# Placing the tiles of a hybrid attention block on multiples of 64 bytes

## Chip, core and metric

The kernel runs on one core of one Trainium2 chip. The metric is the time of one execution on the device in microseconds (us); lower is better. Three executions of the kernel before were timed, and one more was profiled.

## What is computed

One decoder block on 512 tokens of width 2048, in float32. The input is normalised and projected; half of the width goes to eight heads of 128 with compressed, selected and windowed attention (two key and value groups), the other half to sixteen heads of 64 with a window of 128 and an attention sink. Both are gated, projected back, added to the input and normalised.

```python
h = _rmsnorm(x, norm_g[l])
proj = h @ w_in[l]
(qa, kca, vca, ksa, vsa, kwa, vwa, za, ga, qb, kb, vb, zb) = jnp.split(proj, offsets, axis=-1)
...
o_cmp, p_cmp = _compressed_attention(qa, kc, vc)
sel_idx = _select_blocks(p_cmp, S)
o_sel = _selected_attention(qa, _rope(_heads(ksa, N_KV_A, HEAD_DIM_A)), _heads(vsa, N_KV_A, HEAD_DIM_A), sel_idx)
o_win = _banded_attention(qa, _rope(_heads(kwa, N_KV_A, HEAD_DIM_A)), _heads(vwa, N_KV_A, HEAD_DIM_A), WIN_A)
o_a = gates[..., 0:1] * o_cmp + gates[..., 1:2] * o_sel + gates[..., 2:3] * o_win
y_a = o_a.reshape(B, S, WIDTH_A) * jax.nn.silu(za)
o_b = _banded_attention(qb, _rope(_heads(kb, N_KV_B, HEAD_DIM_B)), _heads(vb, N_KV_B, HEAD_DIM_B),
                        WIN_B, sink=sinks[l].reshape(N_KV_B, GROUP_B))
y_b = o_b.reshape(B, S, WIDTH_B) * jax.nn.silu(zb)
x = x + jnp.concatenate([y_a, y_b], axis=-1) @ w_out[l]
return _rmsnorm(x, final_g)
```

With 512 tokens and blocks of 64 there are eight blocks, fewer than the sixteen that are selected, so every block is selected.

## The kernel before

**Three matmuls for one product.** Each float32 operand is split into a rounded word (`hi`, type float32r) and the rest (`lo`). `mm3` forms a product from three float32r matmuls, and these are lines 113 to 115 of the profile:

```python
def mm3(ps, ah, al, bh, bl, first, last, go_on=False):
    pe.matmul(ps, ah, bh, start=first, stop=False, skip_group_check=go_on)
    pe.matmul(ps, ah, bl, start=False, stop=False, skip_group_check=go_on)
    recent["mm"] = pe.matmul(ps, al, bh, start=False, stop=last, skip_group_check=go_on).ins
```

The operand `a` is loaded into TensorE as weights (128 columns), `b` is the moving operand that streams past it. In the profile's names the moving and the loaded operand both stand behind the arrow, moving first: `pj<-xh,whi` streams `xh` past weights `whi`, and `oa<-whi,yh` streams weight words past `yh`.

**Stages.** Weights come from memory by SP's queue into raw tiles (`raw`, 128 x 1024), ScalarE rounds them into `whi` (L89, L616, L913) and VectorE takes the difference into `wlo` (L90, L617, L914); three buffers each. The stages in order of time, with the window that the profile shows:
- to about 96 us: x is loaded, scaled and split into `xh` and `xl` (64 KB a partition in all), and two passes form keys and values to be compressed, and the keys of the other branches, 512 columns a matmul (`bank`, `pj`).
- 96 to 174 us: values token by token, weight words moving in 256 or 408 columns past slices of x, mixed with the two compressions (L228, L229 against the tiles `F`).
- to 201 us: gate and query projections of the first head.
- 201 to 416 us: heads of the first group (`pair` and `attn_a`). A head's query and gate are formed by seven products instead of eight, 256 columns each, from combined tiles `pu`, `xh`, `xl` and, late, halves of the key tiles. In between stand scores (L539), transposes through TensorE (L577, L589, L591), and products with values (L583 to L585).
- 416 to 655 us: the second group, sixteen heads two by two (`qb_evac`, `softmax_b`, `attn_b`): 512-column projections, scores of 256 columns (L820, L821), transposes (L855).
- 655 to 828 us: the output. 512 columns in the first quarter (to 704 us), then for each other quarter seven products of 256 columns with weight words moving past `yh`, `yl` and combinations of them; the raw words of some are summed by a second transfer that accumulates (`ch`, `rw`), or by VectorE (L1072, L1154).

**Order.** A scheduler orders the instructions of each engine by a model of their times, with a few orders fixed by hand (`issue_after`); engines work in that order and wait for each other by semaphores.

**Places in SBUF.** Tiles come from pools that are stacked from the left and from the right end of each partition; a tile's place follows from the sizes opened before it, rounded to 32 bytes. The constants (`ident`, `tab`, `rstd`, `rstdb`, `gates`, `gt`, `eps`) come first, then `wp` with the raw and the split weight words, then `yp` (eight tiles of 4 KB: `F`, `pu`, later the attention's outputs), then work tiles. On the right lie x, and below it keys and values. Three constants have sizes that are no multiple of 64 bytes: `tab` with its single column `rowvalid` at the end (3588 bytes), `rstd` (16) and `eps` (4).

In the built program before, these places follow (bytes from a partition's start, mod 256): weight words 160, `F` and `pu` 160, x and `yh` 224, first key tile (`KH0`, `KL0`) 224, second (`KH1`, `KL1`) 96, `ph` and `pl` 32, queries 160, keys of the second group (`KBH`) 96. All are 32 mod 64.

**Small tiles.** The softmax keeps a minimum (`mn`) and a denominator (`dn`) per row, in the second group also the sink's term (`ex`); each is a tile of 16 or 24 bytes with two buffers.

Of the kernel before, what the change touches and what calls it, by code (L numbers as in the profile page):

```python
# [10 lines left out]
F32 = mybir.dt.float32  # L11
# [6 lines left out]
P = 128  # L18
S = 512
D = 2048  # L20
KT = D // P
NQ = S // P
# [5 lines left out]
CMP = 32  # L28
WARM = 40
FIRST = 1  # L30
TAB_W = 512 + NQ * CMP + 256 + 1


@with_exitstack
def hybrid_block(ctx, tc, xT, xtm, w0, w1s, w2s, wz, wq, wkb, wo0, wos, cw1, cw2, cpos, rope, tabs, sinks, gT, fg, out):
# [3 lines left out]
    def sb(name, bufs=1, side=None):  # L39
        return tc.tile_pool(name=name, bufs=bufs, side=side)  # L40

    const = ctx.enter_context(sb("const"))
    wp = ctx.enter_context(sb("wp", bufs=3))
    ident = const.tile([P, P], F32, name="ident")
    make_identity(nc, ident)
    tab = const.tile([P, TAB_W], F32, name="tab")
    dmask = tab[:, 0:512]
    cmask = tab[:, 512:512 + NQ * CMP]
    bmask = tab[:, 512 + NQ * CMP:768 + NQ * CMP]
    rowvalid = tab[:, TAB_W - 1:TAB_W]  # L50
    rstd = const.tile([P, NQ], F32, name="rstd")
    rstdb = const.tile([P, S], F32, name="rstdb")
    gates = const.tile([P, NQ, 24], F32, name="gates")
    gt = const.tile([P, KT], F32, name="gt")

    def dram(name, *shape):
        return tc.dram_tile(list(shape), F32, name=name)
# [5 lines left out]
    fd = dram("fd", 4, 2, P, KT // 4, 256)  # L63
    fw = dram("fw", 2, 2, P, KT // 4, 256)
    yd = [dram(f"yd{h}", P, S) for h in range(8)]
    eps = const.tile([P, 1], F32, name="eps")
    dve.memset(eps, EPS)
    act.activation(rstd[:, 0:1], eps, AF.Copy)

# [11 lines left out]
    def load_unit(src, width, rawp=None, opening=False):  # L81
# [9 lines left out]
                                       op=ALU.subtract).ins  # L91
        return hi, lo

    xstack = ctx.enter_context(ExitStack())
    xpool = xstack.enter_context(sb("xpool", side="right"))
    xh = xpool.tile([P, KT, S], F32R, name="xh")
# [23 lines left out]
        last["rope"] = dve.tensor_tensor(out=t2[64:128], in0=ps[0:64], in1=sin[0:64], op=ALU.mult).ins  # L120
        return t1, t2

    yp = ctx.enter_context(sb("yp"))
    p0 = ExitStack()
    s0 = p0.enter_context(sb("s0"))
    s0b = p0.enter_context(sb("s0b", bufs=2))
# [376 lines left out]
    wk = wks.enter_context(sb("wk", bufs=2))  # L503
# [8 lines left out]
    sA = ExitStack()  # L512
    pss = sA.enter_context(tc.tile_pool(name="pssA", bufs=1, space=PSUM, side="right"))
    wa = sA.enter_context(sb("wa"))

    def attn_a(h, qh, ql, st):
        g = h // 4
# [2 lines left out]
        pc = wa.tile([P, NQ, 4, CMP], F32, name="pc", tag="pc")  # L520
        for pair in range(2):
            tt = wa.tile([P, 1792 if pair else 768], F32, name=f"tt{pair}", tag=f"tt{pair}")
            mn = wk.tile([P, 2, 3], F32, name="mn", tag="mn")
            dn = wk.tile([P, 2, 3], F32, name="dn", tag="dn")
            views = []
            off = 0
            for i in range(2):
# [221 lines left out]
    psb = ctx.enter_context(ExitStack())  # L749
    pssb = psb.enter_context(tc.tile_pool(name="pssB", bufs=2, space=PSUM, side="right"))  # L750
    wb = wbs.enter_context(sb("wb"))
    cosB, sinB = cosA, sinA
    nc.sync.dma_start(cosB, rope[:, 2, :])
    nc.sync.dma_start(sinB, rope[:, 3, :])
# [48 lines left out]
    def softmax_b(i, q2):  # L803
        g = i // 4
        tts = []
        skb = sk[:, 0, 2 * i:2 * i + 2].unsqueeze(1).to_broadcast([P, 2, 2])
        nskb = sk[:, 1, 2 * i:2 * i + 2].unsqueeze(1).to_broadcast([P, 2, 2])
        for part in range(2):
            mn = wk.tile([P, 2, 2], F32, name="mnb", tag="mnb")
            dn = wk.tile([P, 2, 2], F32, name="dnb", tag="dnb")  # L810
            ex = wk.tile([P, 2, 2], F32, name="exb", tag="exb")
            for e in range(2):
                qt = 2 * part + e
                tt = wb.tile([P, 2, 256], F32, name="ttb", tag="ttb", bufs=6)
                tts.append(tt)
                ko = max(qt - 1, 0) * P
                qs = slice(qt * P, (qt + 1) * P)
                sp = pssb.tile([P, 2, 256], F32, name="spb", tag="spb")
                for v in range(2):
                    pe.matmul(sp[:, v, :], q2[v][:, qs], KBH[:, g, ko:ko + 256], start=v == 0, stop=False)  # L820
                    pe.matmul(sp[:, v, :], q2[v][:, qs], KBL[:, g, ko:ko + 256], start=False, stop=v == 1)  # L821
                n = 256 if qt else 128
                for v in range(2):
                    dve.tensor_tensor_reduce(out=tt[:, v, 0:n], in0=sp[:, v, 0:n], in1=bmask[:, 256 - n:256],
                                             scale=-SCALE_B, scalar=1e38, op0=ALU.add, op1=ALU.min,
                                             accum_out=mn[:, e, v:v + 1])
            dve.tensor_tensor(out=mn, in0=mn, in1=nskb, op=ALU.min)  # L827
            dve.tensor_tensor(out=ex, in0=mn, in1=skb, op=ALU.add)
            act.activation(ex, ex, AF.Exp)
            for e in range(2):  # L830
                n = 256 if part or e else 128
                for v in range(2):
                    tv = tts[2 * part + e][:, v, 0:n]
                    act.activation(tv, tv, AF.Exp, bias=mn[:, e, v:v + 1], scale=-1.0, accum_out=dn[:, e, v:v + 1])  # L834
            dve.tensor_tensor(out=dn, in0=dn, in1=ex, op=ALU.add)
            dve.reciprocal(dn, dn)
            for e in range(2):
                n = 256 if part or e else 128
                for v in range(2):
                    tv = tts[2 * part + e][:, v, 0:n]  # L840
                    dve.tensor_scalar(tv, tv, dn[:, e, v:v + 1], None, op0=ALU.mult)
        return tts
# [404 lines left out]
def _tables():  # L1247
    def rope(d):
        inv = np.float32(10000.0) ** (-np.arange(0, d, 2, dtype=np.float32) / np.float32(d))
        ang = np.arange(S, dtype=np.float32)[None, :] * inv.astype(np.float32)[:, None]  # L1250
        return np.cos(ang.astype(np.float64)).astype(np.float32), np.sin(ang.astype(np.float64)).astype(np.float32)

    ca, sa = rope(128)
    cb, sb_ = rope(64)
    cb, sb_ = np.concatenate([cb, cb]), np.concatenate([sb_, sb_])
    ro = np.stack([np.concatenate([ca, ca]), np.concatenate([sa, -sa]),
                   np.concatenate([cb, cb]), np.concatenate([sb_, -sb_])], axis=1).astype(np.float32)
    p = np.arange(P)[:, None]
    j = np.arange(P)[None, :]
    caus = np.where(j <= p, 0.0, NEG)  # L1260
    band = np.where(j > p, 0.0, NEG)
    c = np.arange(CMP)[None, :]
    cm = [np.where((16 * c + 31 <= q * P + p) & (c < 31), 0.0, NEG) for q in range(NQ)]
    tabs = np.concatenate([np.zeros((P, 384)), caus] + cm + [band, caus, (p >= 31) * 1.0], axis=1).astype(np.float32)
    return np.ascontiguousarray(ro), np.ascontiguousarray(tabs)


# [51 lines left out]
```

## Time and profile before

| | |
|---|---|
| median of 3 executions | 831.02 us (827.9 to 832.21) |
| the profiled execution's own time | 829.19 us |
| its span, first to last instruction | 827.4 us |
| granted TensorE clock, mean | 0.997 |
| TensorE busy | 811.5 us, 98% of the span |
| VectorE, ScalarE, GpSimd busy | 662.1, 485.6 and 89.3 us |
| moved by DMA | 128.30 MB |

A matmul's listed duration runs from its start to its modelled end; the next one starts earlier than that, so durations overlap and the distance between starts is what a matmul costs. Weight loads (PEld) overlap matmuls. An engine's idle time counts only where the chain of work that ended last goes through it.

### The profile page before, as it was taken

To read this page: it belongs to the slowest core of one execution; us is meant where nothing else is said; L and a number is where in the kernel's file an instruction comes from. 1 tells how busy PE (TensorE), PEld (TensorE's weight loads), DVE (VectorE), ACT (ScalarE), POOL (GpSimd) and SP (SyncE) were. 2 spreads that over 40 slices of the span, in tenths; PEclk is the share of its full clock that TensorE was granted. 3 is DMA by queue.
4 is the path that set the end of the run, shared out by engine and by line. 5 is a ranking of instruction groups with operands and counts; after the bars stand their busy time and mean duration, and the time that the engine had idled before them with its cause. 6 is when DMAs were issued, how large, how long until landed. Compare 5 with 4: busy or idle time off the path is not lost.

```text
span 827.4 us, 14161 instructions
## 1 busy us (share of the span) xinstructions
PE 811.5 (98%) x5278; PEld 735.6 (89%) x5278; DVE 662.1 (80%) x1311; ACT 485.6 (59%) x1026; POOL 89.3 (11%) x69
## 2 busy tenths in 40 slices
PE   9999999999999999999999999999999999999996
PEld 7788898999999999999888888888888788999996
DVE  6869786966799898999766688877677798877895
ACT  6734456564676786787665365645444647554555
POOL 3600002011001001101011121011011000110000
PEclk9999999999999999999999999999999999999998
DMA  9665885898330222522733321222222226797845
GB/s 324 194 206 166 281 290 200 265 371 284 103 111 22 99 77 92 166 90 89 251 107 102 99 92 56 74 80 74 77 76 77 77 62 241 235 251 198 244 96 203
DMA packets 52117, 128.30 MB, mean 155 GB/s; under 512 B 4945, under 2 KB 17233, under 8 KB 52049
## 3 DMA queue, kind: packets, MB, share of 16 engines
q1 hardware_dynamic: 50032, 120.59, 43.3%
q0 software_dynamic: 1728, 6.29, 4.3%
q8 instruction: 41, 0.67, 0.3%
q10 hardware_dynamic: 288, 0.52, 0.2%
q14 instruction: 28, 0.22, 0.1%
HBM read 110.31 MB, written 17.07 MB: 154 GB/s over the span
## 4 chain that ended last, share of the span: by engine, by line
PE 84%; DVE 6%; DMA 5%; issue 2%; ACT 2%; SPq 0%; DVEq 0%; ACTq 0%; POOLq 0%
PE pj L115 16%; PE pj L113 15%; PE pj L114 15%; PE bank L115 4%; PE bank L113 4%; PE oa L114 4%; PE oa L113 4%; PE oa L115 3%; PE sp L539 3%; PE bank L114 3%; PE tp L855 2%; DMA rw<-wos 1%; PE tp L577 1%; DMA xr<-xT 1%; DMA raw<-cw 1%
## 5 line engine op out<-in xcount | busy, mean ns | idle before, releaser
L115 PE MATMUL pj<-xh,wlo 128*128 128x512 f32 (+1 forms) x560 | 196.0, 350 | 2.0 <-DVE wlo L617 1.5
L113 PE MATMUL pj<-xh,whi 128*128 128x512 f32 (+1 forms) x560 | 196.2, 350 | 0.8 <-DVE t L665 0.8
L114 PE MATMUL pj<-xl,whi 128*128 128x512 f32 (+1 forms) x560 | 195.4, 349 | 0.0
L90 DVE TENSOR_TENSOR wlo<-raw,whi 128x1024 fp32r<-128x1024 f32 (+2 forms) x102 | 115.3, 1135 | 37.5 <-ACT whi L89 36.6
L89 ACT ACTIVATE whi<-raw 128x1024 fp32r<-128x1024 f32 (+1 forms) x101 | 95.2, 944 | 80.6 <-PE pj L114 24.0
L115 PEld LDWEIGHTS pj<-xh,wlo 128*128 128x128 f32 x560 | 105.3, 188 | 16.3 <-DVE wlo L617 2.2
L113 PEld LDWEIGHTS pj<-xh,whi 128*128 128x128 f32 x560 | 105.4, 188 | 14.2 <-DVE t L665 1.2
L114 PEld LDWEIGHTS pj<-xl,whi 128*128 128x128 f32 x560 | 105.3, 188 | 13.4 <-issue 0.7
L617 DVE TENSOR_TENSOR wlo<-raw,whi 128x1024 fp32r<-128x1024 f32 x49 | 61.6, 1260 | 10.3 <-ACT whi L616 9.9
L616 ACT ACTIVATE whi<-raw 128x1024 fp32r<-128x1024 f32 x49 | 51.7, 1056 | 24.7 <-PE pj L114 12.7
L113 PE MATMUL oa<-whi,yh 128*128 128x256 f32 (+1 forms) x168 | 50.1, 299 | 0.6 <-ACT yh L909 0.6
L114 PE MATMUL oa<-wlo,yh 128*128 128x256 f32 (+1 forms) x168 | 50.4, 300 | 0.2 <-DVE wlo L1147 0.2
L115 PE MATMUL oa<-whi,yl 128*128 128x256 f32 (+1 forms) x168 | 49.7, 299 | 0.0
L834 ACT ACTIVATE ttb<-ttb,mnb 128x256 f32<-128x256 f32 (+1 forms) x64 | 30.1, 471 | 26.0 <-DVE mnb L827 25.5
L509 DVE TENSOR_TENSOR pl<-tp,ph 128x512 fp32r<-128x512 f32 x56 | 37.6, 683 | 6.6 <-ACT ph L508 6.6
L508 ACT ACTIVATE ph<-tp 128x512 fp32r<-128x512 f32 x56 | 32.3, 592 | 17.9 <-PE tp L577 11.2
L114 PE MATMUL bank<-wlo,xh 128*128 128x256 f32 (+1 forms) x128 | 40.2, 316 | 0.0
L115 PE MATMUL bank<-whi,xl 128*128 128x256 f32 (+1 forms) x128 | 39.9, 314 | 0.0
L468 POOL TENSOR_TENSOR t<-t,t 128x512 f32<-128x512 f32 x9 | 19.3, 2147 | 176.4 <-DVE t L120 176.4
L113 PE MATMUL bank<-xh,whi 128*128 128x512 f32 x96 | 37.0, 396 | 1.1 <-ACT whi L89 0.7
L113 PE MATMUL bank<-whi,xh 128*128 128x256 f32 (+1 forms) x128 | 36.7, 318 | 1.3 <-ACT whi L89 1.3
L114 PE MATMUL bank<-xl,whi 128*128 128x512 f32 x96 | 37.0, 391 | 0.0
(356 smaller groups left out, 2202.2 us busy)
## 6 DMA issues: line engine op xcount, KB each, us to landing
raw<-wz SPq DMA_DIRECT2D x36, 512.0 KB, 3.6
raw<-wq SPq DMA_DIRECT2D x28, 512.0 KB, 3.7
raw<-cw SPq DMA_DIRECT2D x16, 512.0 KB, 5.0
raw<-wos SPq DMA_DIRECT2D x12, 512.0 KB, 5.0
rw<-wos SPq DMA_DIRECT2D x10, 512.0 KB, 5.5
xr<-xT SPq DMA_DIRECT2D x16, 256.0 KB, 5.0
raw<-w SPq DMA_DIRECT2D x8, 512.0 KB, 4.2
fd<-ft SPq DMA_DIRECT2D x4, 1024.0 KB, 5.9
```

Source lines behind the costliest of these rows:

```text
L89: last["hi"] = act.activation(hi[:, :width], rw[:, :width], AF.Copy).ins
L90: last["lo"] = dve.tensor_tensor(out=lo[:, :width], in0=rw[:, :width], in1=hi[:, :width].bitcast(F32), op=ALU.subtract).ins
L113: pe.matmul(ps, ah, bh, start=first, stop=False, skip_group_check=go_on)
L114: pe.matmul(ps, ah, bl, start=False, stop=False, skip_group_check=go_on)
L115: recent["mm"] = pe.matmul(ps, al, bh, start=False, stop=last, skip_group_check=go_on).ins
L468: pool.tensor_tensor(out=t1, in0=t1, in1=t2, op=ALU.add)
L508: act.activation(ph, tp, AF.Copy)
L509: dve.tensor_tensor(out=pl, in0=tp, in1=ph.bitcast(F32), op=ALU.subtract)
L539: pe.matmul(sp[:, a:b], qq[:, qs], kk[0][:, ko:ko + b - a], start=pi == 0, stop=pi == 2)
L616: act.activation(hi, src, AF.Copy)
L617: last["lo"] = dve.tensor_tensor(out=lo, in0=src, in1=hi.bitcast(F32), op=ALU.subtract).ins
L834: act.activation(tv, tv, AF.Exp, bias=mn[:, e, v:v + 1], scale=-1.0, accum_out=dn[:, e, v:v + 1])
```

## The change

The tiles behind the constants start on multiples of 64 bytes. `rowvalid` moves from the end of `tab` to the end of `gt`, `rstd` and `eps` share a tile of 32 bytes. The pool `yp` moves from the left to the right end, above x, with a tile of 160 bytes (`edge`) outside it; two unused tiles of 64 bytes (`space`) open the pools of the two attention groups. The small softmax tiles become parts of one tile, `sums`, in both groups.

In the built program after, mod 256: weight words 128, x, `F`, `pu` and `yh` 64, first key tile 64, second 192, `ph` and `pl` 0, queries 128, `KBH` 192. Each engine has the same instructions in the same order as before; ScalarE has two separate semaphore waits fewer, `gt` is loaded with 17 columns for 16, and `tab` with 896 for 897.

```diff
@@ -28,7 +28,7 @@
 CMP = 32
 WARM = 40
 FIRST = 1
-TAB_W = 512 + NQ * CMP + 256 + 1
+TAB_W = 512 + NQ * CMP + 256
 
 
 @with_exitstack
@@ -47,11 +47,12 @@
     dmask = tab[:, 0:512]
     cmask = tab[:, 512:512 + NQ * CMP]
     bmask = tab[:, 512 + NQ * CMP:768 + NQ * CMP]
-    rowvalid = tab[:, TAB_W - 1:TAB_W]
-    rstd = const.tile([P, NQ], F32, name="rstd")
+    small = const.tile([P, 8], F32, name="small")
+    rstd, eps = small[:, 0:NQ], small[:, NQ:NQ + 1]
     rstdb = const.tile([P, S], F32, name="rstdb")
     gates = const.tile([P, NQ, 24], F32, name="gates")
-    gt = const.tile([P, KT], F32, name="gt")
+    gt = const.tile([P, KT + 1], F32, name="gt")
+    rowvalid = gt[:, KT:KT + 1]
 
     def dram(name, *shape):
         return tc.dram_tile(list(shape), F32, name=name)
@@ -63,7 +64,6 @@
     fd = dram("fd", 4, 2, P, KT // 4, 256)
     fw = dram("fw", 2, 2, P, KT // 4, 256)
     yd = [dram(f"yd{h}", P, S) for h in range(8)]
-    eps = const.tile([P, 1], F32, name="eps")
     dve.memset(eps, EPS)
     act.activation(rstd[:, 0:1], eps, AF.Copy)
 
@@ -91,6 +91,9 @@
                                        op=ALU.subtract).ins
         return hi, lo
 
+    edge = ctx.enter_context(sb("edge", side="right"))
+    edge.tile([P, 40], F32, name="edge")
+    yp = ctx.enter_context(sb("yp", side="right"))
     xstack = ctx.enter_context(ExitStack())
     xpool = xstack.enter_context(sb("xpool", side="right"))
     xh = xpool.tile([P, KT, S], F32R, name="xh")
@@ -120,7 +123,6 @@
         last["rope"] = dve.tensor_tensor(out=t2[64:128], in0=ps[0:64], in1=sin[0:64], op=ALU.mult).ins
         return t1, t2
 
-    yp = ctx.enter_context(sb("yp"))
     p0 = ExitStack()
     s0 = p0.enter_context(sb("s0"))
     s0b = p0.enter_context(sb("s0b", bufs=2))
@@ -512,6 +514,7 @@
     sA = ExitStack()
     pss = sA.enter_context(tc.tile_pool(name="pssA", bufs=1, space=PSUM, side="right"))
     wa = sA.enter_context(sb("wa"))
+    wa.tile([P, 16], F32, name="space")
 
     def attn_a(h, qh, ql, st):
         g = h // 4
@@ -520,8 +523,8 @@
         pc = wa.tile([P, NQ, 4, CMP], F32, name="pc", tag="pc")
         for pair in range(2):
             tt = wa.tile([P, 1792 if pair else 768], F32, name=f"tt{pair}", tag=f"tt{pair}")
-            mn = wk.tile([P, 2, 3], F32, name="mn", tag="mn")
-            dn = wk.tile([P, 2, 3], F32, name="dn", tag="dn")
+            sums = wk.tile([P, 2, 2, 3], F32, name="sums", tag="sums")
+            mn, dn = sums[:, 0], sums[:, 1]
             views = []
             off = 0
             for i in range(2):
@@ -749,6 +752,7 @@
     psb = ctx.enter_context(ExitStack())
     pssb = psb.enter_context(tc.tile_pool(name="pssB", bufs=2, space=PSUM, side="right"))
     wb = wbs.enter_context(sb("wb"))
+    wb.tile([P, 16], F32, name="space")
     cosB, sinB = cosA, sinA
     nc.sync.dma_start(cosB, rope[:, 2, :])
     nc.sync.dma_start(sinB, rope[:, 3, :])
@@ -806,9 +810,8 @@
         skb = sk[:, 0, 2 * i:2 * i + 2].unsqueeze(1).to_broadcast([P, 2, 2])
         nskb = sk[:, 1, 2 * i:2 * i + 2].unsqueeze(1).to_broadcast([P, 2, 2])
         for part in range(2):
-            mn = wk.tile([P, 2, 2], F32, name="mnb", tag="mnb")
-            dn = wk.tile([P, 2, 2], F32, name="dnb", tag="dnb")
-            ex = wk.tile([P, 2, 2], F32, name="exb", tag="exb")
+            sums = wk.tile([P, 3, 2, 2], F32, name="sums", tag="sums")
+            mn, dn, ex = sums[:, 0], sums[:, 1], sums[:, 2]
             for e in range(2):
                 qt = 2 * part + e
                 tt = wb.tile([P, 2, 256], F32, name="ttb", tag="ttb", bufs=6)
@@ -1261,7 +1264,7 @@
     band = np.where(j > p, 0.0, NEG)
     c = np.arange(CMP)[None, :]
     cm = [np.where((16 * c + 31 <= q * P + p) & (c < 31), 0.0, NEG) for q in range(NQ)]
-    tabs = np.concatenate([np.zeros((P, 384)), caus] + cm + [band, caus, (p >= 31) * 1.0], axis=1).astype(np.float32)
+    tabs = np.concatenate([np.zeros((P, 384)), caus] + cm + [band, caus], axis=1).astype(np.float32)
     return np.ascontiguousarray(ro), np.ascontiguousarray(tabs)
 
 
@@ -1304,7 +1307,7 @@
         "rope": ro,
         "tabs": tabs,
         "sinks": np.broadcast_to(a["sinks"][0][None, :], (P, 16)),
-        "gT": a["norm_g"][0].reshape(KT, P).T,
+        "gT": np.concatenate([a["norm_g"][0].reshape(KT, P).T, (np.arange(P)[:, None] >= 31).astype(np.float32)], axis=1),
         "fg": np.broadcast_to(a["final_g"][None, :], (P, D)),
     }
     arrays = {k: np.ascontiguousarray(v) for k, v in arrays.items()}
```

## The prediction

> **What bounds the kernel now.** I read the page first.
>
> ```profile
> span 827.4 us, 14161 instructions
> PE 811.5 (98%) x5278; PEld 735.6 (89%) x5278; DVE 662.1 (80%) x1311; ACT 485.6 (59%) x1026; POOL 89.3 (11%) x69
> PEclk9999999999999999999999999999999999999998
> PE 84%; DVE 6%; DMA 5%; issue 2%; ACT 2%; SPq 0%; DVEq 0%; ACTq 0%; POOLq 0%
> ```
>
> TensorE is busy 98% of the span at a steady granted clock, and the chain that ends last is 84% matmul. A cheaper step counts as far as it shortens the spacing of the matmuls, or lets another engine become late. So the second view is the table of stretches, cut at the kernel's stages; after those, two stretches that hold one shape almost alone.
>
> ```profile
> 0.00:21.00 21.00, 19.43 (x107) 16.12 (x108) 14.12 (x21) 13.57 (x22) 8.46 (x12) 1.00 0.91 325
> 21.00:96.00 75.00, 74.18 (x325) 60.07 (x324) 61.35 (x86) 37.87 (x59) 13.56 (x10) 1.00 0.60 198
> 96.00:201.00 105.00, 103.31 (x656) 97.45 (x656) 75.89 (x125) 59.51 (x105) 11.00 (x10) 1.00 0.84 289
> 201.00:416.00 215.00, 211.53 (x1707) 206.00 (x1706) 187.81 (x408) 155.98 (x381) 20.12 (x13) 1.00 0.35 115
> 416.00:655.00 239.00, 239.00 (x1260) 201.79 (x1259) 180.19 (x453) 123.61 (x300) 25.48 (x13) 1.00 0.25 81
> 655.00:697.00 42.00, 41.44 (x192) 33.48 (x191) 38.74 (x79) 25.82 (x49) 0.00 (x0) 1.00 0.33 102
> 697.00:755.00 58.00, 58.00 (x479) 56.51 (x478) 45.24 (x61) 33.01 (x57) 5.41 (x6) 1.00 0.84 254
> 755.00:828.00 73.00, 64.59 (x565) 64.20 (x563) 58.78 (x82) 36.25 (x57) 5.22 (x6) 0.97 0.64 181
> 52.70:96.40 43.70, 43.70 (x193) 35.88 (x193) 40.04 (x66) 18.27 (x29) 0.00 (x0) 1.00 0.54 174
> 685.70:704.50 18.80, 18.80 (x83) 15.17 (x82) 16.02 (x41) 14.99 (x36) 1.62 (x2) 1.00 0.74 269
> 704.60:803.80 99.20, 99.20 (x877) 99.20 (x876) 83.16 (x94) 50.06 (x67) 8.92 (x11) 1.00 0.77 208
> ```
>
> The columns are window, length, then busy time and count of PE, weight load, DVE, ACT and POOL, the clock, the DMA share and GB/s. Matmuls overlap, so what one costs is its distance to the next. That is the stretch plus one matmul's duration, divided by the count.
>
> ```profile
> L113 PE MATMUL pj<-xh,whi 128*128 128x512 f32 x336 | 132.9, 396 | 0.4 <-DVE t L665 0.4
> L113 PE MATMUL bank<-xh,whi 128*128 128x512 f32 x96 | 37.0, 396 | 1.1 <-ACT whi L89 0.7 <-ACT xh L139 0.3
> L113 PE MATMUL oa<-whi,yh 128*128 128x256 f32 x136 | 37.5, 276 | 0.0
> L114 PE MATMUL bank<-wlo,xh 128*128 128x256 f32 x64 | 17.8, 283 | 0.0
> L114 PE MATMUL bank<-wlo,xh 128*128 128x408 f32 x64 | 22.4, 349 | 0.0
> L577 PE MATMUL tp<-ident,tt 128*128 128x128 f32 x128 | 21.6, 272 | 0.0
> L855 PE MATMUL tp<-ident,ttb 128*128 128x128 f32 x112 | 16.9, 273 | 0.0
> ```
>
> 512 columns (52.7 to 96.4 us): (43.70 + 0.396) / 193 = 228.5 ns. 256 columns in the last products (704.6 to 803.8): (99.20 + 0.276) / 877 = 113.4 ns. The timeline gives 256 columns elsewhere, first and last of seven successive matmuls each:
>
> ```profile
> 201.82 0.28 PE L113 MATMUL pj<-pu,whi 128*128 128x256 f32 x1
> ...
> 202.54 0.28 PE L113 MATMUL pj<-pu,whi 128*128 128x256 f32 x1
> 207.32 0.28 PE L114 MATMUL pj<-xl,whi 128*128 128x256 f32 x1
> ...
> 208.03 0.28 PE L114 MATMUL pj<-xl,whi 128*128 128x256 f32 x1
> ```
>
> Six steps in 0.72 us are 120 ns, and six in 0.71 us are 118 ns. The same shape costs 113, 118 and 120 ns at the same clock, in runs without a wait. What differs is which tiles are read, and so their addresses.
>
> **Reading the addresses.** In the program before, every operand of a three-term product lies 32 bytes past a multiple of 64 (x at 224 mod 256, weight words at 160, `pu` at 160). A moving row of 256 float32 is 1024 bytes. From such a start it touches 17 blocks of 64 bytes, where 16 would do; 512 columns touch 33 instead of 32. If TensorE takes one block at a time at its full rate, a block costs 113.4 / 17 = 6.67 ns. Then 118 and 120 ns are 17.7 and 18 blocks, and 228.5 ns is 34.3: the extra part of a block is then a clash of the moving read with the weight load that runs beside it (equal addresses mod 256, `pu` against `whi`, are the worst). This is a hypothesis: no matmul before that streams at this rate has whole blocks. The 408-column ones touch 26 blocks from either start, so they are no test and gain nothing.
>
> **The change, part by part.** The built programs hold the same instructions in the same order on every engine; only places differ. Weight words move to 128 mod 256; x, `pu`, `yh` and the first key tile to 64; `ph` and `pl` to 0; the second key tile, KBH and VB to 192. Everything in a three-term product is then on a multiple of 64.
>
> *One block less in each matmul.* Per stage, count times 6.67 ns, the transposes (x128 and x112) and the 192 of 408 columns taken off, smaller odd groups left in (under 2 us too much):
> - 0 to 21 us: nothing. These rows of the chain show that transfers set the pace there:
>
> ```profile
> 2.62 4.81 DMA xr<-xT
> 7.50 6.46 DMA xr<-xT
> 14.02 7.13 DMA raw<-w
> 117.51 8.37 DMA raw<-cw
> 764.71 2.27 DVE ch L1072 x2
> 775.22 7.02 DMA rw<-wos
> 792.48 5.23 DMA rw<-wos
> ```
>
> - 21 to 96: 325 x 6.67 = 2.2 us, all of it, since DVE (61 of 75) keeps up.
> - 96 to 201: 464 x 6.67 = 3.1. DMA is at 0.84 and the chain waits 8.4 us for `cw`; I count half, 1.5.
> - 201 to 416: 1579 x 6.67 = 10.5. DVE is at 187.8 of 215 and TensorE already idles 3.5 us; at 205 us DVE would be at 92%. I count 80%, 8.4.
> - 416 to 655: 1148 x 6.67 = 7.7, all: TensorE is never idle and DVE is at 75%.
> - 655 to 697: 192 x 6.67 = 1.3; DVE is at 92%, so half, 0.6.
> - 697 to 755: 479 x 6.67 = 3.2. The weight load runs 56.5 of 58 us and may bind before 106.7 ns is reached; two thirds, 2.1.
> - 755 to 828: 565 x 6.67 = 3.8, but the chain there goes through `ch`, `rw` and DVE (the last rows above). A quarter, 0.9.
>
> Sum: 2.2 + 1.5 + 8.4 + 7.7 + 0.6 + 2.1 + 0.9 = 23.4 us. The two ends for a block are 0 and 6.67 ns; I take the upper one, since 113.4 is the least spacing over 877 matmuls and divides into 17 whole blocks.
>
> *The relation mod 256.* Before, a matmul with moving x has its weights 64 below x; after, 64 above. With moving weight words it is the reverse. The 512-column matmuls of the output (weights 64 above) take (18.80 + 0.396) / 83 = 231 ns against 228.5, and the 256-column ones 113.4 against 118. But `bank<-wlo,xh` has the very relation of the last products and lasts 283 ns, not 276. So the relation moves a matmul by -4.4 to +3 ns and doesn't fix it; I take zero, and keep both ends in the rivals.
>
> *Small tiles.* Minimum, denominator and sink terms share one tile per pair of query tiles, so the next-but-one use waits for the last reader of all of them. Those readers stand ahead of it on DVE and ACT anyway, and ACT loses two separate semaphore waits. `rowvalid` comes with `gt`, in a first transfer that is 4 bytes a partition longer. Zero for both: if the cover failed, one wait per pair would be a DVE step behind an idle PSUM bank, well under 1 us in all. DVE, ACT and transfers work at the new places too; nothing here shows whether their speed depends on the place, and off the path it would count only through the fractions above.
>
> The sum goes against the profiled execution's 829.19 us (span 827.4): 805.8. That execution is 1.8 us below the median of 831.02, so the forecast is 807.6, rounded to 807 us.
>
> By the Trainium skill's page "SBUF — State Buffer", section "Door 1: The DMA port swizzle", a line is 16 bytes; 32 mod 64 is on such a line already, and by that alone the first term is nothing. By its "TensorE: Matmul & The Clock Gate", section "Wait — 56ns, not 53.3ns?", a warm matmul takes N / 2.4 + 2.5 ns, 109.2 and 215.8 here, an estimate that the trace misses by 4 to 13 ns; by it there is room for the whole gain and more.
>
> **The rivals.**
> - *Clashes go as well.* If the new relation also frees the moving read of clashes, 512 columns come to 32 blocks, 213.3 ns: 228.5 - 213.3 - 6.67 = 8.5 ns more for 3 x (336 + 96) = 1296 matmuls, 11.0 us, and 256 columns of the middle stage 118 - 106.7 - 6.67 = 4.6 ns more for 1579, 7.3 us. DVE at 92% in the middle and transfers leave about 13 of 18.3: 794 us. For it: 113.4 shows that a clash-free state exists. Against it: no 512-column stretch came near 220.
> - *Blocks don't matter.* The 113.4 is 256 columns and a fixed overhead, and only the clashes differ. Then about 831 us stays, and one says that the change does nothing for the time. It fits every spacing above as well, except that 17 whole blocks is then chance. The Trainium skill's 16-byte line is this rival.
> - *Only the relation counts, and the wrong way.* The place: every 512-column matmul with moving x gets weights 64 above, 231.3 for 228.5, 2.8 x 1296 = 3.6 us; every 256-column one of the last products gets them 64 below, 118 for 113.4, 4.6 x 1044 = 4.8 us. Sum 8.4: 840 us. It decides where the block saved is below some 2 ns. For it: both spacings stand in rows. Against: the 283 ns row.
>
> **How the numbers follow.** Forecast 0.50, clashes gone 0.14, nothing 0.15, slower by relation 0.21. A difference under 0.5% (4 us) can't be told from none here. Faster 0.65 (the forecast and the first rival, with a little of the forecast's case coming out near nothing), same 0.14, slower 0.21. The range reaches from 790, just under the first rival, to 835, past no change, and leaves out the slow rival's 840 and little below: 790 to 835. The likeliest case's own range is 798 to 820: the fractions of the stages all one quarter higher or a half lower.
>
> **What would show it.** Right: 52.7 to 96.4's kind of stretch at about 222 ns a matmul, the last products at 107 to 110, the run of `pu` under 114; durations of 276 down to about 270; TensorE's idle time in the middle stage up by 1 to 2 us; the chain richer in DVE and DMA. Wrong: 276 and 113.4 unchanged in the last products (blocks don't matter), 118 there (the relation rules), or spacing down but the end not (another engine was as late all along).

## The result, and the profile after

The kernel after takes 833.2 us in the median (832.1 to 834.56, 20 executions), the kernel before 831.68 in the same comparison (827.9 to 833.68, 20 executions). The ratio is 1.0026, with a 95% interval of 1.0015 to 1.0036: slower by a quarter of a per cent, 26 us above the forecast. It lies inside the forecast's range only because the range was drawn past no change at its upper end. The after's profiled execution took 832.67 us, 3.5 more than the one before.

From the page of the kernel after: span, busy times, granted clock, and the chain that ended last.

```profile
span 830.9 us, 14159 instructions
PE 816.4 (98%) x5278; PEld 738.0 (89%) x5278; DVE 663.8 (80%) x1311; ACT 485.4 (58%) x1026; POOL 90.5 (11%) x69
PEclk9999999999999999999999999999999999999998
PE 89%; DVE 4%; ACT 2%; DMA 2%; issue 1%; SPq 0%; DVEq 0%; ACTq 0%
```

The clock is the same, and TensorE grew most: 811.5 to 816.4 us busy, VectorE by 1.7. The forecast looked for a chain richer in DVE and DMA; it became richer in PE, 84% to 89%, and DMA fell from 5% to 2%. So TensorE got slower, not faster. Where, the table of stretches tells (columns as before; the last two rows lie inside runs of one shape).

```profile
0.00:21.00 21.00, 19.84 (x104) 16.75 (x105) 15.81 (x22) 14.05 (x23) 9.73 (x12) 1.00 0.92 331
21.00:96.00 75.00, 75.00 (x325) 60.18 (x324) 61.01 (x86) 37.23 (x58) 13.01 (x10) 1.00 0.62 197
96.00:201.00 105.00, 103.71 (x659) 97.57 (x658) 75.99 (x125) 59.36 (x105) 11.06 (x10) 1.00 0.85 289
201.00:416.00 215.00, 211.12 (x1718) 205.30 (x1717) 189.11 (x410) 155.79 (x381) 21.52 (x14) 1.00 0.35 115
416.00:655.00 239.00, 239.00 (x1246) 199.70 (x1245) 178.99 (x452) 123.45 (x300) 24.49 (x13) 1.00 0.26 81
655.00:697.00 42.00, 41.44 (x195) 33.92 (x194) 38.86 (x79) 26.35 (x49) 0.00 (x0) 1.00 0.35 102
697.00:755.00 58.00, 57.95 (x463) 56.41 (x461) 43.38 (x59) 32.37 (x55) 5.41 (x6) 1.00 0.85 253
54.00:94.00 40.00, 40.00 (x173) 32.23 (x172) 38.97 (x65) 16.60 (x27) 0.00 (x0) 1.00 0.52 171
725.00:800.00 75.00, 75.00 (x640) 75.00 (x639) 61.20 (x69) 36.37 (x48) 7.25 (x9) 1.00 0.77 208
```

Read the counts of matmuls (first bracket). Up to 697 us they add up to 104 + 325 + 659 + 1718 + 1246 + 195 = 4247, and before to 107 + 325 + 656 + 1707 + 1260 + 192 = 4247: at 697 us both kernels stand at the same matmul. The second group lost 14 matmuls of progress (1260 to 1246), the first group won 11, the other stages 3. After 697 the kernel falls behind: 463 for 479 in the first 58 us, and the matmul that starts at 803.87 us before starts at 807.52 after. This lag of 3.65 us is what becomes the 3.5.

The spacing says why. 512 columns: (40.00 + 0.397) / 173 = 233.5 ns, where before had 228.5. Last products: (75.00 + 0.279) / 640 = 117.6 ns, where before had 113.4. The durations tell the same, in the groups by shape:

```profile
L116 PE MATMUL pj<-xh,whi 128*128 128x512 f32 x336 | 133.4, 397 | 0.5 <-DVE t L668 0.5
L116 PE MATMUL oa<-whi,yh 128*128 128x256 f32 x136 | 37.9, 279 | 0.0
L116 PE MATMUL pj<-pu,whi 128*128 128x256 f32 x112 | 31.9, 285 | 0.0
```

396 became 397, 276 became 279, and `pu`, 287 before, got 2 ns shorter. None fell by a block's 6.67 ns.

### The profile page after: what moved, and what is told of

It reads as the page before. It is cut to its first block, busy times and chain, and to the rows that moved or that the text cites. A ratio compares the mean times of both kernels' runs of the same rounds, so it can differ in the third digit from the quotient of the medians.

```text
span 830.9 us, 14159 instructions
## 1 busy us (share of the span) xinstructions
PE 816.4 (98%) x5278; PEld 738.0 (89%) x5278; DVE 663.8 (80%) x1311; ACT 485.4 (58%) x1026; POOL 90.5 (11%) x69
## 4 chain that ended last, share of the span: by engine, by line
PE 89%; DVE 4%; ACT 2%; DMA 2%; issue 1%; SPq 0%; DVEq 0%; ACTq 0%
PE pj L118 15%; PE pj L117 15%; PE pj L116 15%; PE bank L116 5%; PE bank L118 5%; PE bank L117 5%; PE oa L117 4%; PE oa L116 4%; PE oa L118 4%; PE sp L542 3%; PE tp L858 1%; PE tp L580 1%; PE spb L823 1%; DMA raw<-cw 1%; PE spb L824 1%
## 5 line engine op out<-in xcount | busy, mean ns | idle before, releaser
L90 DVE TENSOR_TENSOR wlo<-raw,whi 128x1024 fp32r<-128x1024 f32 (+2 forms) x102 | 115.9, 1141 | 33.1 <-ACT whi L89 30.8
L837 ACT ACTIVATE ttb<-ttb,sums 128x256 f32<-128x256 f32 (+1 forms) x64 | 30.1, 471 | 25.1 <-DVE sums L830 24.6
```

The lines of the kernel that those rows point to most:

```text
L90: last["lo"] = dve.tensor_tensor(out=lo[:, :width], in0=rw[:, :width], in1=hi[:, :width].bitcast(F32), op=ALU.subtract).ins
```

## Experiments

All spacings below are start to start. In the whole kernel I read them from one stretch each of 512 columns with moving x (54 to 94 us) and of 256 columns in the last products (725 to 800), as above; one matmul more or less in the count is 1.3 ns in the first and 0.2 in the second. *Distance* is the place of the weights less the place of the moving words, mod 256. Moving x has distance 192 before and 64 after, the last products the reverse.

**1. Back to the old distance, with and without multiples of 64; and a third distance.** All start from the kernel after.

```diff
# x192_w128: old distances, multiples of 64
-    edge.tile([P, 40], F32, name="edge")
+    edge.tile([P, 8], F32, name="edge")
# x224_w160: old distances, 32 past a multiple of 64, as before
+    const.tile([P, 8], F32, name="pad")
     small = const.tile([P, 8], F32, name="small")
...
-    edge.tile([P, 40], F32, name="edge")
# x0_w128: distance 128 in both, multiples of 64
-    edge.tile([P, 40], F32, name="edge")
+    edge.tile([P, 56], F32, name="edge")
...
-    wa.tile([P, 16], F32, name="space")
...
-    wb.tile([P, 16], F32, name="space")
```

> The changed kernel with the outer tile of 32 bytes for 160: x, pu and yh at 192 mod 256, weight words at 128, so weights 64 below a moving x as in the kernel before, and everything in a three-term product still on a multiple of 64. Theory R (the spacing of the matmuls goes by the place of the weights against the moving words, mod 256, and not by blocks of 64): as the kernel before, 831 us within 2, the 512-column projections at 229 ns for the changed kernel's 233.5, the last products at 113.4 ns for 117.9. Rival B (blocks of 64 do save 6.67 ns a matmul, and the turned relation took it back): 831 - 23 = 808 us, 512 columns near 222 ns, last products near 107 to 109. Rival N (places do not matter, the rest is chance): as the changed kernel, 833 us, 233.5 and 117.9 ns.

> The changed kernel with a tile of 32 bytes ahead of the weight words and no outer tile: x at 224 mod 256, weight words at 160, the very places of the kernel before (all 32 past a multiple of 64), with the changed kernel's pools and joined small tiles. R: equal to the run with x at 192 and w at 128 within 2 us, 229 and 113.4 ns. B: slower than that run by some 23 us, 831 us. N: 833 us, 233.5 and 117.9 ns.

> The changed kernel with an outer tile of 224 bytes and without the two unused tiles of 64: x, pu and yh at 0 mod 256, weight words at 128, half the period apart either way. R: a spacing of its own, the same for moving x and for moving weight words of one width, since 128 above is 128 below; between the clash-free 33 slots and the worst seen, 220 to 236 ns for 512 columns and 113 to 120 for 256; 815 to 840 us. B and N: as the changed kernel, 833 us within 2.

The two stretches of x192_w128, and then of x224_w160:

```profile
54.00:94.00 40.00, 40.00 (x177) 32.81 (x176) 38.19 (x65) 16.39 (x26) 0.00 (x0) 1.00 0.53 174
725.00:800.00 75.00, 75.00 (x640) 75.00 (x638) 61.18 (x70) 36.66 (x48) 6.98 (x8) 1.00 0.76 208
```

```profile
54.00:94.00 40.00, 40.00 (x176) 32.81 (x175) 38.74 (x65) 16.44 (x26) 0.00 (x0) 1.00 0.52 172
725.00:800.00 75.00, 75.00 (x664) 75.00 (x663) 63.51 (x71) 36.99 (x49) 7.36 (x9) 1.00 0.79 215
```

x192_w128: 829.52 us, ratio to before 0.9992 (0.9971 to 1.0013). x224_w160: 828.18, 0.9977 (0.996 to 0.9995). x0_w128: 837.06, 1.0087 (1.0054 to 1.0121). The 512 columns follow the distance: 228 to 229.5 ns at 192 on either kind of start (177 and 176 in 40 us), 233.5 at 64, and at 128 (40.00 + 0.396) / 174 = 232.2. Multiples of 64 gave them nothing. But the last products, at distance 64 in both of the first two, took 117.6 ns on multiples of 64 and 113.4 on the others. So the distance alone does not fix that spacing.

**2. Distance by itself.** 48 matmuls a setting, nothing else at work: weights `b` bytes into one tile, moving words `a` into another; *even* starts the moving words on a multiple of 64, *odd* 32 past one, *back* goes through the distances in falling order.

```python
for i in range(48):
    pe.matmul(t[:, 0:n], w[:, b // 4:b // 4 + 128], x[:, a // 4:a // 4 + n], start=i == 0, stop=i == 47)
```

> Only matmuls on two tiles, 48 back to back for each setting, nothing waits; the block's work is left out. Full is 512 moving columns, half 256; even starts the moving words on a multiple of 64 bytes, odd 32 past one; the number is how many bytes mod 256 the weight words lie above the moving ones; back repeats even in falling order. R: even and odd agree for each distance within 1 ns a matmul; full 64 gives 233, full 192 gives 229, half 64 gives 113.4 or 117.8, half 192 117.8, half zero 120. B: odd is 6.67 ns above even at every distance. N: all settings of one width agree within 1 ns. None of the three says what 32, 96, 128, 160 and 224 give.

Groups by name of this run, busy us and mean ns at the end. Spacing is (busy - mean) / 47, to 1 ns or so by the rounding: the last row is (5.6 - 0.276) / 47 = 113 ns.

```profile
L36 PE MATMUL full_even_zero<-x,w 128*128 128x512 f32 x48 | 11.1, 390 | 0.0
L36 PE MATMUL full_odd_zero<-x,w 128*128 128x512 f32 x48 | 11.1, 390 | 0.0
L36 PE MATMUL full_even_sixtyfour<-x,w 128*128 128x512 f32 x48 | 11.4, 396 | 0.0
L36 PE MATMUL full_odd_sixtyfour<-x,w 128*128 128x512 f32 x48 | 11.4, 396 | 0.0
L36 PE MATMUL full_even_oneninetytwo<-x,w 128*128 128x512 f32 x48 | 11.2, 392 | 0.0
L36 PE MATMUL full_back_oneninetytwo<-x,w 128*128 128x512 f32 x48 | 11.4, 398 | 0.0
L36 PE MATMUL half_even_zero<-x,w 128*128 128x256 f32 x48 | 5.9, 283 | 0.0
L36 PE MATMUL half_odd_zero<-x,w 128*128 128x256 f32 x48 | 5.9, 283 | 0.0
L36 PE MATMUL half_even_sixtyfour<-x,w 128*128 128x256 f32 x48 | 5.8, 281 | 0.0
L36 PE MATMUL half_odd_sixtyfour<-x,w 128*128 128x256 f32 x48 | 5.8, 281 | 0.0
L36 PE MATMUL half_back_sixtyfour<-x,w 128*128 128x256 f32 x48 | 5.6, 276 | 0.0
```

Read from the last twelve steps, start to start, of each group, in ns:

| distance | 0 | 32 | 64 | 96 | 128 | 160 | 192 | 224 |
|---|---|---|---|---|---|---|---|---|
| 512 columns | 226.7 | 233.3 | 233.3 | 234.6 | 232.8 | 233.3 | 228.9 or 233.3 | 233.3 |
| 256 columns | 120.0 | 118.2 | 113.3 or 117.8 | 117.5 | 118.8 | 120.0 | 117.8 | 117.8 |

Even and odd starts agree to 0.1 ns at every distance. A block of 64 bytes touched or not touched costs nothing. The distance moves a matmul of 512 columns by up to 8 ns, one of 256 by up to 7, with its least at another place for each width. And at two of these settings the same distance has two spacings, each held to the end of its group. Four of the values in the table, 113.3, 120.0, 226.7 and 233.3 ns, are 17, 18, 34 and 35 times 6.67 ns: the step from which the prediction started is there, but how many steps a matmul takes does not go with the blocks that it touches.

**3. Only the attention's outputs moved; and what the effect needs.** In yh192_w128 `yh` and `yl` go 128 bytes down, so the last products get distance 64 and everything ahead stays as after. The map repeats the bare run with more distances, fewer weight columns, other widths and bfloat16.

```diff
# yh192_w128
             yl = [so1.tile([P, S], F32R, name=f"yl{f}") for f in range(16)]
+            so1.tile([P, 32], F32, name="space")
```

> The changed kernel with one unused tile of 128 bytes in the pool of the output's operands: yh, yl and their combinations at 192 mod 256 for 64, so that they, as weights, lie 64 above the moving weight words (at 128), as in the kernel before; all else as in the changed kernel. Theory R (the spacing goes by the distance from the moving words to the weights, mod 256): the last products back from 117.9 to 113.4 ns, 4.5 x about 900 = 4.0 us, and the 512-column products of the output from 229 to 233, 4 x 190 = 0.8 us the other way: 3.2 us off the changed kernel's time, ratio to the kernel before 0.998 to 0.999 if all of it reaches the end; less if transfers and VectorE are late there as they were in the chain before. Rival P (the last products lost their 4.5 ns by the pools' new order or the joined tiles, not by the distance): 117.9 ns stays, ratio 1.0026.

> Only matmuls, 24 back to back for each setting, nothing waits; the block's work is left out. Full is 512 moving columns, half 256, up and down go through all distances in steps of 8 bytes in both orders; quarterload, halfload and mostload load 32, 64 and 96 weight columns for 128; wide are other numbers of moving columns; sixteenbit is bfloat16. Theory C (the spread over distances is a clash of the moving read with the weight load beside it): with 32 weight columns the distances agree within 1 ns, and full is 220 or less; the more columns, the wider the spread; with 16-bit words, half the reads, little or no spread. Rival F (a fixed cost for each matmul that goes by its start alone): the spread with 32 columns is the same as with 128. On the blocks: even and odd agree with 32 columns too, as they did with 128. Expected of the map: full best near zero and 240 at 226.7, 233 elsewhere, and two values (228.8 and 233.3) at 192 by what went before; half 113.3 or 117.8 at 64 by what went before, 120 at zero and 160.

yh192_w128 took 832.52 us, 1.0019 (1.0 to 1.0037). Its last products, and then rows of the map: bfloat16 at distances 0 and 64, and 64 weight columns at distance 0.

```profile
725.00:800.00 75.00, 75.00 (x640) 75.00 (x639) 60.84 (x70) 36.83 (x48) 7.85 (x9) 1.00 0.77 211
```

```profile
L53 PE MATMUL sixteenbit_full_zero<-xb,wb 128*128 128x512 bf16 x24 | 5.4, 379 | 0.0
L53 PE MATMUL ixteenbit_full_sixtyfour<-xb,wb 128*128 128x512 bf16 x24 | 5.3, 379 | 0.0
L53 PE MATMUL halfload_full_even_zero<-x,w 128*64 128x512 f32 x24 | 5.7, 392 | 0.0
```

The last products stayed at 117.6: distance 64 allows 113.3 and does not bring it. That is what rival P said would be seen, but its reason, the pools' new order or the joined tiles, is ruled out by x224_w160, which has both and took 113.4. In bfloat16 each of the four distances gave 215.8 ns (512) and 109.2 (256). The Trainium skill, "TensorE: Matmul & The Clock Gate", section "Wait — 56ns, not 53.3ns?", gives N / 2.4 + 2.5 ns, 215.8 and 109.2: that agrees exactly there, and not for this kernel's float32r. Theory C is borne out only in part. At 512 moving columns the spread over the four distances and both starts was 1.7 ns with 32 weight columns (230.0 to 231.7), 4.8 with 64, and 6.7 with 96 and with 128, so it shrinks with the weight columns; but the level with 32 did not fall to 220 or less. Even and odd starts, which theory C and rival F alike took to agree, did not everywhere with fewer weight columns: at 256 moving and 32 weight columns, distance 0, they took 113.3 and 117.8 ns, each in one group.

The map, in steps of 8 bytes, also has more distances with several spacings: 512 columns took 226.7 or 233.3 ns at 40 and 226.7 or 231.9 at 216, and 256 columns 113.3 or 116.7 at 88. At 240, where the run called distances had 226.7 ns, the map had 228.3 twice. Other widths differ in how much the distance matters: 448 columns took 206.7, 202.3 and 200.0 ns at 0, 64 and 192, and 320 columns 146.7 or 146.8 at all three. What happens inside the chip stays open.

**4. The distance of the least 512-column spacing.** x, `pu` and `yh` at 128 put distance 0 into all; the second kernel puts `yh` at 192 besides.

```diff
# both
-    edge.tile([P, 40], F32, name="edge")
+    edge.tile([P, 24], F32, name="edge")
# x128_yh192
             yl = [so1.tile([P, S], F32R, name=f"yl{f}") for f in range(16)]
+            so1.tile([P, 48], F32, name="space")
```

> The outer unused tile is 96 bytes, for 160: x, pu and yh start at 128 mod 256, as the weight words do, so the distance from the moving words to the weights is 0 in the products with x and in the last ones. If spacing follows the distance alone, as in the run of matmuls without other work: 512 columns 226.7 ns (after 233.8, before 229.4), 256 columns 119 to 120 ns in the last products (before 113.4). Then 1250 x -2.7 = -3.4 us and 1000 x +6 = +6.0 us against before, +2 to +3 us in all: 832.5 to 834. If the distances measured without other engines at work do not carry over into the kernel: 512 columns at 229 or more.

> As x128_w128, with an unused tile of 192 bytes behind yl, which puts yh and yl at 192 mod 256: distance 0 for the 512 columns with x, 64 for the last products. Distance rule: 512 columns 226.7 ns (-3.4 us against before); the 256 columns with moving x 119 to 120 ns for 117.7 (some 400 to 700 of them, +1 to +1.5 us); the last products at either of their two spacings, 113.4 (nothing against before, time 829 to 831) or 117.8 (+4 us, 833 to 835). If the time follows the sum of the spacings by about half, as in the five programs so far, the ends come closer: 830 to 833.

x128_w128 took 832.32 us, 1.0024 (1.0006 to 1.0041); x128_yh192 829.38, 0.9985 (0.9966 to 1.0004). The stretches of x128_w128, and the last products of x128_yh192:

```profile
54.00:94.00 40.00, 40.00 (x178) 33.16 (x177) 38.34 (x65) 16.44 (x26) 0.00 (x0) 1.00 0.53 175
725.00:800.00 75.00, 75.00 (x627) 75.00 (x626) 60.50 (x69) 36.22 (x48) 6.96 (x8) 1.00 0.76 208
```

```profile
725.00:800.00 75.00, 75.00 (x639) 75.00 (x639) 61.18 (x70) 37.03 (x48) 6.96 (x8) 1.00 0.78 208
```

(40.00 + 0.390) / 178 = 226.9 ns and (75.00 + 0.283) / 627 = 120.1 ns: the bare run's 226.7 and 120.0 carry over into the kernel at work, in both widths and in opposite directions. The time of x128_w128 is 0.2 us under the expectation's range. For x128_yh192 the distance rule asked for 833 to 835 with last products at 117.8, or 830 to 833 if only half of the sum reached the end, and the time was 829.4: a sum of spacings in one trace does not give the time to better than a few us.

**5. The same distances 32 bytes higher.** An unused tile of 32 bytes ahead of the constants, and an outer tile 32 bytes shorter, move every tile of a product off the multiples of 64, to starts 32 past one as before.

```diff
# x160_yh224: x128_yh192 moved up; x96_yh224: yh192_w128 moved up (its edge goes from 40 to 32)
+    const.tile([P, 8], F32, name="pad")
     small = const.tile([P, 8], F32, name="small")
...
-    edge.tile([P, 24], F32, name="edge")
+    edge.tile([P, 16], F32, name="edge")
```

> x128_yh192 with every tile of a product 32 bytes higher, as in the program before (an unused tile of 32 bytes ahead of the constants, the outer one 64 bytes): the same distances, but all starts 32 past a multiple of 64. So far the last products at distance 64 came at 117.8 ns in the three programs on multiples of 64 and at 113.4 in the two 32 bytes past one. Theory S (a start 32 past decides which of the two spacings is taken): 113.4 ns, 4 us less than x128_yh192 in the last stage, 825 to 827 us, the fastest of all. Theory E (what runs ahead decides, the start does not matter): 117.8, and x128_yh192's 829.4 again within 1 us.

> yh192_w128 with every tile of a product 32 bytes higher in the same way. Theory S: last products 113.4 ns for 117.8, 828 to 830 us where yh192_w128 took 832.5. Theory E: 117.8, 832 to 833 us. In both, 512 columns with x at 233 to 234 ns.

The last products of x160_yh224, then of x96_yh224:

```profile
725.00:800.00 75.00, 75.00 (x664) 75.00 (x663) 63.25 (x73) 37.10 (x49) 6.96 (x8) 1.00 0.78 213
```

```profile
725.00:800.00 75.00, 75.00 (x664) 75.00 (x663) 62.93 (x71) 36.87 (x48) 8.71 (x10) 1.00 0.78 212
```

Both at 113.4 ns, as theory S said; part 6 has other runs of the same traces that speak against it. The times: 828.88 us, 0.9974 (0.9958 to 0.999), and 831.55, 1.0005 (0.9991 to 1.0018). Both lie above what theory S put (825 to 827 and 828 to 830). They are about 1 us less than their partners on multiples of 64, not the 4 us that the spacing promised, and the intervals overlap. x160_yh224 is, with x224_w160, the fastest of all: both beat the kernel before by a quarter of a per cent, and neither lies on multiples of 64. Their intervals overlap those of x128_yh192 and x192_w128, which do.

**6. The change with the multiples of 64 taken out; and what picks one of two spacings.** x96_w160 has after's distances and before's starts. In the bare run called entries, groups of 36 matmuls stand at a distance with two spacings, each behind another run of 20 to 22 matmuls.

```diff
# x96_w160
+    const.tile([P, 8], F32, name="pad")
     small = const.tile([P, 8], F32, name="small")
...
-    edge.tile([P, 40], F32, name="edge")
+    edge.tile([P, 32], F32, name="edge")
```

> The kernel after, with every tile of a product 32 bytes higher (an unused tile of 32 bytes ahead of the constants, the outer one 128 bytes): after's distances, before's starts 32 past a multiple of 64. If the multiples of 64 themselves do nothing at these distances (the run of bare matmuls gave one spacing at distance 192 for both starts, 117.75 ns): last products 117.8 to 117.9, 512 columns with x 233.8, and after's time within 1 us, 832 to 834. If the start also decides here: last products at 113.4, 829 to 830.

> Only matmuls; the block's work is left out. 16 times each, groups of 36 matmuls at a distance with two spacings (256 columns at 64; 512 columns at 192), for starts on a multiple of 64 (even) and 32 past one (odd), each time behind another run of 20 to 22 matmuls of another distance and width. If the start decides by itself: odd groups at 113.3 ns for 256 columns, all or nearly all, even ones at 117.8. If what runs ahead decides: each of the 16 entries gives the same spacing for even and for odd, some 113.3 and some 117.8. If neither, a mixture that does not pair.

x96_w160 took 833.55 us, 1.0039 (1.0022 to 1.0056), and after 1.0026 (1.0015 to 1.0036). Its stretches, then groups of entries:

```profile
54.00:94.00 40.00, 40.00 (x173) 32.08 (x172) 38.62 (x65) 16.57 (x26) 0.00 (x0) 1.00 0.52 174
725.00:800.00 75.00, 75.00 (x639) 75.00 (x638) 61.53 (x69) 36.04 (x48) 7.29 (x9) 1.00 0.78 211
```

```profile
L36 PE MATMUL half_even_c<-x,w 128*128 128x256 f32 x36 | 4.4, 281 | 0.0
L36 PE MATMUL half_odd_c<-x,w 128*128 128x256 f32 x36 | 4.3, 276 | 0.0
L36 PE MATMUL half_even_l<-x,w 128*128 128x256 f32 x36 | 4.3, 277 | 0.0
L36 PE MATMUL half_odd_l<-x,w 128*128 128x256 f32 x36 | 4.4, 281 | 0.0
```

x96_w160 has after's spacings (173 in 40 us; 639 in 75) and after's time within the intervals. This is the test of the change itself: with the distances of after, the multiples of 64 are worth nothing that shows.

In entries, a group's duration tells its spacing: 276 or 277 goes with 113.3 ns, 281 with 117.8. 6 of 16 even groups and 9 of 16 odd ones took the lower, and not in pairs: behind the same prelude *c* only odd, behind *l* only even. So in the bare run neither the start nor the prelude's distance and width decides by itself; the exact moment of entry may. The 512 columns at distance 192 took 228.9 ns in 30 of their 32 groups and 233.3 in two, one even and one odd.

In the kernel, the last products of the four programs with distance 64 and odd starts showed 113.4, those of the three on multiples of 64 117.6 to 117.8, each in one profiled execution. Other runs at distance 64 in the same traces show that the start does not decide there either. Between 95 and 127 us, weight words move past slices of x in eight runs of 22 or 24 matmuls. Before (odd) took 113.3 ns in two of them and 117.8 in six, x192_w128 (even) 113.3 in six and 117.8 in two, x224_w160 (odd) 113.3 in all eight. Here is one of them, the same 21 matmuls, first and last, in before and in x192_w128:

```profile
112.32 0.28 PE L114 MATMUL bank<-wlo,xh 128*128 128x256 f32 x1
...
114.68 0.28 PE L114 MATMUL bank<-wlo,xh 128*128 128x256 f32 x1
111.05 0.28 PE L117 MATMUL bank<-wlo,xh 128*128 128x256 f32 x1
...
113.32 0.28 PE L117 MATMUL bank<-wlo,xh 128*128 128x256 f32 x1
```

Twenty steps take 2.36 us on an odd start and 2.27 on an even one, the reverse of theory S. With moving x or `pu` at distance 64 in the first group, counting runs of 12 matmuls or more, 13 end at 113.3 and 15 at 117.8 in after (even), 14 and 17 in x96_yh224 (odd); the rest mix both. So the seven last products may owe their spacing to how each was entered; what picks it is open.

Only one execution of each kernel was traced. If the others differ in this, a gain of 113.3 over 117.8 in one trace reaches the median only in part. It fits that kernels without distance 64 in the last products scatter less: standard deviations of 0.57 us (after, 20 executions), 0.66 (x0_w128, 4), 1.03 (x128_w128, 10) and 1.18 (x96_w160, 12), against 1.38 to 1.87 for before in its six comparisons and 1.14 to 2.09 for the others. The two ranges overlap, so that is an argument, not a showing.

All kernels together, sorted by distance. The spacings here run from the first start to the last in the same two stretches, which takes out the error of counting at the ends (the 117.6 above is 117.8 here); each agrees within 0.5 ns with what the bare run gave for its distance:

| kernel | distance, moving x / last products | 512 columns | last products | time, ratio to before |
|---|---|---|---|---|
| x160_yh224 | 0 / 64, odd | 226.7 | 113.3 | 0.9974 |
| x128_yh192 | 0 / 64, even | 226.7 | 117.8 | 0.9985 |
| x128_w128 | 0 / 0, even | 226.7 | 120.0 | 1.0024 |
| x224_w160 | 192 / 64, odd | 228.9 | 113.3 | 0.9977 |
| before | 192 / 64, odd | 228.9 | 113.3 | 1 |
| x192_w128 | 192 / 64, even | 228.9 | 117.8 | 0.9992 |
| x96_yh224 | 64 / 64, odd | 233.3 | 113.3 | 1.0005 |
| yh192_w128 | 64 / 64, even | 233.3 | 117.8 | 1.0019 |
| x96_w160 | 64 / 192, odd | 233.3 | 117.8 | 1.0039 |
| after | 64 / 192, even | 233.3 | 117.8 | 1.0026 |
| x0_w128 | 128 / 128, even | 232.3 | 118.7 | 1.0087 |

## Why the prediction was wrong

**The step that failed** is "The two ends for a block are 0 and 6.67 ns; I take the upper one, since 113.4 is the least spacing over 877 matmuls and divides into 17 whole blocks." The term was 23.4 us and measured nothing: even and odd starts agree at every distance in the bare run with 128 weight columns, the kernel's number, x192_w128 and x224_w160 have the same 512-column spacing, and x96_w160 has after's time. After, with 32 blocks touched in place of 33, a matmul of 512 columns takes 233.5 ns. The 113.4 came back from starts on a multiple of 64 too (`half_back_sixtyfour`, even), where 16 blocks are touched: its 17 steps of 6.67 ns are not blocks. The rule beside it, the 16-byte line of the Trainium skill's "SBUF — State Buffer", section "Door 1: The DMA port swizzle", asked for nothing from this term, and that is what came.

**The second step** is "the relation moves a matmul by -4.4 to +3 ns and doesn't fix it; I take zero". Its first half was right and its conclusion was not. The row against it, 283 ns for `bank<-wlo,xh` with the last products' own relation, is a mean over runs with both spacings of that distance, two at 113.3 and six at 117.8 ns: a distance sets which spacings are possible, sometimes two. The rival built on it, *Only the relation counts, and the wrong way*, was the case that happened: it put 231.3 ns for the 512 columns, measured 233.5 (read start to start, the output's 512 columns before took 233.2 already; one matmul more or less among the 83 counted is 2.8 ns); it put 118 for the last products, measured 117.6. Its total of 8.4 us was too big. The 3.6 us of the 512 columns never reached the end. Up to 697 us the lost progress of the second group was given back by the first group (11 matmuls), the stage bound by transfers and the output's first quarter (3 each); one part of this is the first group's 256 columns with moving x and `pu`, at distances 192 and 0 before and both at 64 after: the mean step fell from 117.7 to 115.9 ns with x and from 119.3 to 116.1 with `pu`, since some runs took 113.3. Between 21 and 96 us TensorE had 0.8 us of idle time (74.18 busy of 75.00) and has none now. Of the last products' 4.8 us, 3.5 reached the end of the profiled execution and 1.5 the median. In the profile before TensorE ran ahead there until VectorE was late by half a microsecond; two successive matmuls of its timeline, with the wait at the end of the row:

```profile
803.87 0.28 PE L113 MATMUL oa<-whi,yh 128*128 128x256 f32 x1
804.38 0.39 PE L114 MATMUL oa<-wlo,yh 128*128 128x256 f32 x1 [0.24 <-DVE wlo L1147]
```

After, the matmuls run on without a gap to 811.76 us, and the chain that went through `ch`, `rw` and VectorE before goes from matmul to matmul (many steps left out):

```profile
780.24 0.12 PE pj L117
...
790.84 0.12 PE oa L117
...
801.44 0.12 PE oa L117
```

Of the other rivals, *Blocks don't matter* was right on the blocks and missed the distance, and *Clashes go as well* has no ground: no distance brought 512 columns under 226.7 ns. Idle time in the middle stage, asked to rise by 1 to 2 us, went from 3.5 to 3.9.

**What held.** Order and clock are unchanged. The small tiles and the move of `yp` cost nothing that shows: x224_w160 has them, with before's places for x and weights, and is no slower (0.996 to 0.9995). Its small gain may come from `pu`, now at distance 192, with a mean step of 117.6 ns in place of 119.3, and from weight words moving past x, 113.5 in place of 116.9. The 408 columns stayed where they were but for 0.9 ns (186.5 to 185.6). The reading of the stages, that only 416 to 655 us and parts of the others follow TensorE in full, was not put to a test by this change, as the spacing did not fall.

## What to carry to other kernels

A regular number (17 steps of 6.67 ns) that fits a mechanism is no evidence for it while another reading fits as well: a bare run of matmuls, with the start and the distance as its only variables, would have told the two apart before any tile was moved. Where TensorE is busy 98% of the time in float32r, try the place of the weights against the moving words mod 256, and not their alignment; the best distance is another one for each width, and moving one tile for one stage changes it for the others. The gain is small: the best of the ten kernels here won a quarter of a per cent. And take a price from several profiled executions where a spacing can have two values.

## What was not expected of the hardware

- The spacing of float32r matmuls depends on the distance mod 256 between weights and moving words: 226.7 to 234.6 ns at 512 columns, 113.3 to 120.0 at 256 (up to 122.4 in the map), clock 1.00. bfloat16 shows none of it at four distances (215.8 and 109.2).
- Matmuls of one form at one distance can run at one of two spacings, in the last products for hundreds on end: 113.3 or 117.8 ns (256 columns, distance 64). In groups of 36 or 48, 512 columns at distance 192 took 228.9 or 233.3.
- In the bare runs a matmul's listed duration is its spacing plus 161 to 165 ns (276 and 113.3; 283 and 120.0; 390 and 226.7; 396 and 233.3), so a difference of durations there tells a difference of spacing. In the whole kernel it is less sure: `pj<-pu,whi` after has 285 with a mean step of 116.1, since means mix runs and waits.
